# Two edits in the output stage of a gated encoder layer: which queue issues some stores, and where some loads stand in the queue

## The chip, the cores and the metric

The kernel runs on one core of a Trainium2 chip. The metric is the time of one execution in microseconds (us), lower is better. The time before is the median of three executions.

A core has a matrix engine (PE, with its weight loads shown as PEld), a vector engine (DVE), a scalar engine (ACT), GpSimd (POOL) and SyncE (SP). Each engine works off its own list of instructions in order. A DMA transfer is issued by an instruction in such a list: the engine that issues it waits until the data and the buffer are ready, and everything behind it in the same list waits too. The transfers themselves run on 16 DMA engines.

## The reference

One encoder layer over 1024 rows of width 2048. What matters here is its end: the merged branches times the output weights, a row norm, a gain, and the sum with the input.

```python
o = merged @ w_out                                   # (1024, 2048) @ (2048, 2048)
return x + gate[:, None] * rmsnorm(o, post_g)        # rmsnorm: rows scaled by 1 / sqrt(mean of squares + eps)
```

All is float32. Each matmul operand is split into a high and a low half, and three products stand for one. The squares of a whole row of `o` are needed before any element of the row can be finished.

## The kernel before

The large matmuls are done by a Strassen scheme of seven products for each 2x2 arrangement of blocks. The last stage, the output stage, is four calls of `out_pair(half, i, op, between, after)`: `half` is the half of the rows (rows 0 to 511, then 512 to 1023), and `i` picks a 512-wide column block out of each half of the columns. So each call makes, in seven products, the blocks of four row tiles (T, 128 rows each) by two column blocks (n). The calls come in the order (0,0), (0,1), (1,0), (1,1). One product is 48 matmuls of 128x512.

The weights of a product come in four loads of 512 KB (`wr`, L1185 for sums of weights kept in scratch, L1188 for `w_out` itself), into a ring of four buffers. A buffer is free again when its two halves have been split by ACT (`whi`, L95) and DVE (`wlo`, L96). So each product's weights are loaded about one product ahead. All of these loads are issued by SP.

A finished block is multiplied by the gain on DVE (L1284) in `result`. Of the calls for the first half, (0,1) keeps its eight blocks in SBUF (`held`), and (0,0) puts its eight blocks into a scratch tensor `o_d` (store at L1288, eight stores of 256 KB).

When a row's squares are complete, the rows of the first half are finished during (1,0) and the beginning of (1,1). `first_rows(T, n)` gives two steps for each of 16 blocks: `fetch` loads the block back from `o_d` if it is not held (L1353, eight loads `mo<-o_d`), and the block of `x` (L1220); `put_out` has DVE compute the final block in place (L1215) and stores it to the output (L1216). The tiles of these steps are a ring of eight places, used in turn: the blocks that come from `o_d` take the places 0, 2, 4, 6 and again 0, 2, 4, 6, so that a later load into a place must wait until the earlier block in that place has been stored. The steps are called from `between_10` and `between_11`, twice in each product; a step calls `fetch` of one block and then `put_out` of the block two earlier. The blocks of the second half are finished by `third_block` and at the very end of (1,1), with `finish_block` too.

The order of instructions within one engine's list is not the order of the code: a scheduler simulates the program and puts an instruction into its engine's list when it takes its inputs and buffers to be ready, earlier code first. `keep(ins)` (L90) is the exception: it adds an order without a wait, so that `ins` stands in its engine's list behind the instruction that the code traced last on that engine. It sets only this lower bound.

In the code, `load` and `store` are both `nc.sync.dma_start`, so loads and stores stand in the one list of SP.

Of the kernel before, what the change touches and what calls it, by code (L numbers as in the profile page):

```python
# [20 lines left out]
P = 128  # L21
# [21 lines left out]
def encoder_layer(ctx: ExitStack, tc: tile.TileContext, x, c, table, w_ada, b_ada, pre_g,  # L43
# [15 lines left out]
    nc = tc.nc  # L59
# [30 lines left out]
    def keep(ins):  # L90

        tc.keep_in_program_order(ins)
# [14 lines left out]
    load = nc.sync.dma_start  # L107
    store = nc.sync.dma_start
# [24 lines left out]
    o_d = dram.tile([S // 2, D], F32, name="o_d")  # L133
# [218 lines left out]
    for r0, src in ((0, c[0]), (16, b_ada[0, 0:D]), (32, b_ada[0, D:2 * D]),  # L352
                    (48, pre_g[0]), (64, b_merge[0]), (96, pool_scale[0])):
        n = src.shape[0] // P
# [421 lines left out]
    held = {}  # L776
# [421 lines left out]
    xrow, held = {}, {}  # L1198

    def rows_of(T, n):  # L1200
        return out[T * P:(T + 1) * P, n * 512:(n + 1) * 512]

    def square(src, T, n):
        nc.scalar.activation(bank("at", "junk"), src, AF.Square, accum_out=ssq[:, T, n:n + 1])

    def row_scale(T):
        s_ = const.tile([P, 3], F32, tag="st", name=uid("st"), bufs=4)
        nc.vector.tensor_reduce(s_[:, 0:1], ssq[:, T], op=ALU.add, axis=AX.X)
        nc.scalar.activation(s_[:, 1:2], s_[:, 0:1], AF.Sqrt, bias=eps_t, scale=1.0 / D)
        nc.vector.reciprocal(s_[:, 2:3], s_[:, 1:2])  # L1210
        return s_[:, 2:3]

    def finish_block(T, n, scale):
        r = held.pop((T, n))
        keep(nc.vector.scalar_tensor_tensor(r, r, scale, xrow.pop((T, n)), op0=ALU.mult, op1=ALU.add))  # L1215
        store(rows_of(T, n), r)  # L1216

    def fetch_x_block(T, n, tile_of):
        xrow[T, n] = tile_of("xr")
        load(xrow[T, n], x[T * P:(T + 1) * P, n * 512:(n + 1) * 512])  # L1220
# [7 lines left out]
    def out_pair(half, i, op, between, after=None):  # L1228
# [50 lines left out]
        def result(blk, t, src, dst):  # L1279

            T, nh = half * 4 + (int(blk[1]) - 1) * 2 + t, int(blk[0]) - 1
            n = 2 * nh + i
            square(src, T, n)
            nc.vector.tensor_tensor(dst, src, g[nh], ALU.mult)  # L1284
            if stays:
                held[T, n] = dst
            else:
                store(o_d[T * P:(T + 1) * P, n * 512:(n + 1) * 512], dst)  # L1288

        def kept(tag):  # L1290

# [14 lines left out]
        for t in range(2):  # L1306
            result("11", t, bx[t], c11[t])
        product("A22", "T4", bv)
        for t in range(2):
            add(u2[t], bv[t], u2[t])  # L1310
            result("21", t, u2[t], u2[t])
# [7 lines left out]
        for t in range(2):  # L1319
            add(p7[t], p7[t], u4[t])  # L1320
            result("22", t, p7[t], p7[t])
# [8 lines left out]
        for t in range(2):  # L1330
            for j, w in enumerate(ws):
                out_mm(bz[t], op, "B22", j, t, w, False, j == len(ws) - 1)
            result("12", t, bz[t], c12[t])
            scale = row_scale(6 + t)
            for n in (0, 2, 3, 1):
                finish_block(6 + t, n, scale)

    nextm, nextt2 = [], {}
    scales = {}
# [4 lines left out]
    def first_rows(T, n):  # L1344

        def place(name):
            ring.rotate(-1)
            return ring[-1]

        def fetch():  # L1350
            if (T, n) not in held:
                held[T, n] = place("fo")
                load(held[T, n], o_d[T * P:(T + 1) * P, n * 512:(n + 1) * 512])  # L1353
            fetch_x_block(T, n, place)

        def put_out():
            if T not in scales:
                scales[T] = row_scale(T)
            finish_block(T, n, scales[T])

        return fetch, put_out

# [52 lines left out]
    def third_block():  # L1415
        assert not side
        for T in (4, 5):
            scale = row_scale(T)
            for b in range(4):
                finish_block(T, b, scale)  # L1420
# [43 lines left out]
```

## Time and profile before

| | |
|---|---|
| median of 3 executions | 2125.57 us (2125.16 to 2127.92) |
| the profiled execution | 2127.43 us, its span 2125.6 us |
| PE busy | 2091.7 us, 98% of the span |
| DVE, ACT busy | 1537.8 us, 1109.0 us |
| POOL busy | 7.5 us |
| output stage | from about 1812 us to the end |
| DMA issues of the stage that the change touches | 8 stores to `o_d`, 8 loads from it, 16 stores of first-half blocks |

Times in the profile count from the start of the span. A line of the timeline has the start, the duration, the engine, the line of the kernel, the operation, and what it writes and reads. "SPq" is SP's list: the row of a DMA there is its issue and not its transfer; a DMA that had to wait is shown where it was issued at last. A bracket [0.96 <-ACT whi L95] is idle time of the engine before the instruction and what ended it. In the view of waits, "SPq L1353 <- DMA out_dram<-mo" reads: SP stood at line 1353 until a transfer from `mo` to the output had landed; then the sum, the number of times, and the longest.

### The profile page before, as it was taken

How to read it: one execution, taken by the hardware profiler on the slowest of the kernel's cores; microseconds unless marked ns; L12 is line 12 of the kernel's file. 1: busy time of each engine (PE TensorE's matmuls, PEld its weight loads, DVE VectorE, ACT ScalarE, POOL GpSimd, SP SyncE). 2: the span in 40 equal slices, each digit the busy share in tenths (PEclk: the TensorE clock that was granted, in tenths of full speed). 3: DMA queues.
4: the chain of work that ended last, by engine and by line, in shares of the span. 5: the costliest groups of instructions: out<-in, count | busy, mean ns of one | idle time of the engine just before them, and what ended most of it. 6: DMA issues, size and time to landing. Idle time of an engine off the chain costs nothing.

```text
span 2125.6 us, 28919 instructions
## 1 busy us (share of the span) xinstructions
PE 2091.7 (98%) x9567; PEld 1715.3 (81%) x9567; DVE 1537.8 (72%) x2754; ACT 1109.0 (52%) x2102; POOL 7.5 (0%) x66
## 2 busy tenths in 40 slices
PE   6999999999999999999999999999999999999998
PEld 4588888887888888888888888888788888878876
DVE  5786667777547676677777678866957977879667
ACT  5654444444474544665655544333645644768554
POOL 0000000000000000000000000000000000000000
PEclk9999999999999999999999999999999999999999
DMA  9886566899676356544545476666745556686896
GB/s 328 272 269 216 186 207 222 303 307 318 223 232 204 122 177 204 169 158 161 198 148 166 151 243 226 212 219 193 249 157 173 174 200 201 227 291 223 299 311 233
DMA packets 303254, 466.10 MB, mean 219 GB/s; under 512 B 23882, under 2 KB 144866, under 8 KB 303104
## 3 DMA queue, kind: packets, MB, share of 16 engines
q1 hardware_dynamic: 301648, 462.02, 65.9%
q0 software_dynamic: 1120, 2.19, 0.3%
q8 instruction: 75, 1.23, 0.2%
q14 instruction: 75, 0.61, 0.1%
q10 hardware_dynamic: 336, 0.06, 0.0%
HBM read 340.41 MB, written 125.85 MB: 219 GB/s over the span
## 4 chain that ended last, share of the span: by engine, by line
PE 87%; DVE 5%; DMA 5%; issue 1%; ACT 1%; SPq 0%; ACTq 0%; DVEq 0%
PE Z L235 29%; PE V L235 19%; PE X L235 19%; DMA raw<-in_w_merge_dram 2%; PE Z L1194 2%; PE Z L1195 2%; PE Z L1196 2%; PE V L1194 1%; PE V L1196 1%; PE V L1195 1%; PE GEMV L455 1%; DVE wlo L96 1%; PE X L1194 1%; PE X L1196 1%; PE X L1195 1%
## 5 line engine op out<-in xcount | busy, mean ns | idle before, releaser
L95 ACT ACTIVATE whi<-raw 128x512 fp32r<-128x512 f32 (+1 forms) x528 | 321.8, 610 | 527.1 <-PE Z L235 262.3
L96 DVE TENSOR_TENSOR wlo<-raw,whi 128x512 fp32r<-128x512 f32 (+1 forms) x528 | 347.6, 662 | 164.3 <-PE Z L235 129.2
L96 DVE TENSOR_TENSOR wlo<-wr,whi 128x512 fp32r<-128x512 f32 x224 | 151.3, 689 | 62.3 <-ACT whi L95 59.7
L95 ACT ACTIVATE whi<-wr 128x512 fp32r<-128x512 f32 x224 | 138.7, 629 | 96.4 <-DVE wlo L96 33.5
L102 DVE TENSOR_TENSOR raw<-raw,raw 128x512 f32<-128x512 f32 x80 | 55.2, 691 | 106.6 <-DMA raw<-in_w_merge_dram 78.2
L235 PE MATMUL V<-T3h,whi 128*128 128x512 f32 x336 | 92.1, 393 | 0.5 <-DVE u L102 0.5
L235 PE MATMUL V<-T4l,whi 128*128 128x512 f32 x336 | 91.2, 390 | 0.9 <-DVE T4l L96 0.8
L235 PE MATMUL X<-B11h,whi 128*128 128x512 f32 x336 | 92.0, 392 | 0.0
L235 PE MATMUL Z<-T2h,whi 128*128 128x512 f32 x336 | 91.6, 392 | 0.1
L95 ACT ACTIVATE whi<-ws 128x512 fp32r<-128x512 f32 (+1 forms) x88 | 53.7, 611 | 72.6 <-PE X L235 66.5
L235 PE MATMUL Z<-T1h,whi 128*128 128x512 f32 x336 | 91.6, 390 | 0.0
L235 PE MATMUL Z<-B22h,whi 128*128 128x512 f32 x336 | 91.6, 392 | 0.0
L235 PE MATMUL X<-B21h,whi 128*128 128x512 f32 x336 | 91.2, 391 | 0.0
L235 PE MATMUL V<-T4h,whi 128*128 128x512 f32 x336 | 91.2, 391 | 0.0
L235 PE MATMUL Z<-T2h,wlo 128*128 128x512 f32 x336 | 90.8, 390 | 0.2 <-DVE wlo L96 0.2
L235 PE MATMUL X<-B11l,whi 128*128 128x512 f32 x336 | 90.9, 390 | 0.0
L235 PE MATMUL Z<-T1l,whi 128*128 128x512 f32 x336 | 90.8, 390 | 0.0
L235 PE MATMUL Z<-B22l,whi 128*128 128x512 f32 x336 | 90.7, 390 | 0.0
L235 PE MATMUL X<-B11h,wlo 128*128 128x512 f32 x336 | 90.7, 390 | 0.0
L235 PE MATMUL V<-T3l,whi 128*128 128x512 f32 x336 | 90.7, 390 | 0.0
L235 PE MATMUL X<-B21l,whi 128*128 128x512 f32 x336 | 90.6, 389 | 0.0
L235 PE MATMUL Z<-T1h,wlo 128*128 128x512 f32 x336 | 90.6, 389 | 0.0
(308 smaller groups left out, 4811.8 us busy)
## 6 DMA issues: line engine op xcount, KB each, us to landing
part<-part_d SPq DMA_DIRECT2D x136, 256.0 KB, 4.8
ada<-in_w_ada_dram SPq DMA_DIRECT2D x128, 256.0 KB, 5.4
raw<-in_w_in_dram SPq DMA_DIRECT2D x64, 512.0 KB, 4.0
raw<-in_w_merge_dram SPq DMA_DIRECT2D x64, 512.0 KB, 5.7
wr<-ws_dS SPq DMA_DIRECT2D x64, 512.0 KB, 5.2
wr<-in_w_out_dram SPq DMA_DIRECT2D x48, 512.0 KB, 5.2
proj_d<-part SPq DMA_DIRECT2D x68, 256.0 KB, 2.2
sw<-in_w_out_dram SPq DMA_DIRECT2D x64, 256.0 KB, 5.5
```

The costliest lines, as they stand in the source:

```text
L95: ins = (nc.scalar.activation(hi, src, AF.Copy), nc.vector.tensor_tensor(lo, src, f32(hi), ALU.subtract))
L96: nc.vector.tensor_tensor(lo, src, f32(hi), ALU.subtract))
L102: return (eng or nc.vector).tensor_tensor(o, a, b, ALU.add)
L235: nc.tensor.matmul(ps, w_[:, i], op[mov][j][m_], start=fresh and i == 0 and n == 0, stop=i == nj - 1 and n == 2, skip_group_check=True)
L455: ins = nc.tensor.matmul(pv[g:g + 32, :], scz[:, kc, :], tile_of(kc), start=kc < 4, stop=kc >= 12, tile_position=(0, g))
L1194: nc.tensor.matmul(pb, hi, w[0], start=first, stop=False, skip_group_check=True)
L1195: nc.tensor.matmul(pb, lo, w[0], start=False, stop=False, skip_group_check=True)
L1196: nc.tensor.matmul(pb, hi, w[1], start=False, stop=last, skip_group_check=True)
```

## The change

The diff has three parts.

- The eight stores of `result` to `o_d` are issued by GpSimd and not by SP.
- `finish_block` takes the store as an argument. `put_out` of `first_rows` passes GpSimd's, so the 16 stores of first-half blocks go to GpSimd too. The other callers, `third_block` and the end of (1,1), keep SP.
- The eight loads from `o_d` in `fetch` get `keep`: each stands in SP's list behind the instruction traced just before it on SP. The blocks of `x` beside them are loaded as before, without it.

```diff
-    def finish_block(T, n, scale):
+    def finish_block(T, n, scale, store=store):
         r = held.pop((T, n))
         keep(nc.vector.scalar_tensor_tensor(r, r, scale, xrow.pop((T, n)), op0=ALU.mult, op1=ALU.add))
         store(rows_of(T, n), r)
...
             if stays:
                 held[T, n] = dst
             else:
-                store(o_d[T * P:(T + 1) * P, n * 512:(n + 1) * 512], dst)
+                nc.gpsimd.dma_start(o_d[T * P:(T + 1) * P, n * 512:(n + 1) * 512], dst)
...
             if (T, n) not in held:
                 held[T, n] = place("fo")
-                load(held[T, n], o_d[T * P:(T + 1) * P, n * 512:(n + 1) * 512])
+                keep(load(held[T, n], o_d[T * P:(T + 1) * P, n * 512:(n + 1) * 512]))
             fetch_x_block(T, n, place)
...
             if T not in scales:
                 scales[T] = row_scale(T)
-            finish_block(T, n, scales[T])
+            finish_block(T, n, scales[T], nc.gpsimd.dma_start)
```

## The prediction

> **What bounds the kernel now.** I read the page first, then the engines' timeline in the output stage, then the waits of SP's list and the chain.
>
> ```profile
> span 2125.6 us, 28919 instructions
> PE 2091.7 (98%) x9567; PEld 1715.3 (81%) x9567; DVE 1537.8 (72%) x2754; ACT 1109.0 (52%) x2102; POOL 7.5 (0%) x66
> ```
>
> PE is the bound. An edit outside the matmuls can win only what PE stands still, or what follows its last matmul. In the output stage the timeline of PE shows three such places:
>
> ```profile
> 1893.58 0.39 PE L1196 MATMUL X<-wlo,mh 128*128 128x512 f32 x1
> 1895.34 0.50 PE L1194 MATMUL V<-whi,mh 128*128 128x512 f32 x1 [1.37 <-ACT whi L95]
> ...
> 2050.63 0.39 PE L1195 MATMUL V<-whi,ml 128*128 128x512 f32 x1
> 2050.86 0.39 PE L1196 MATMUL V<-wlo,mh 128*128 128x512 f32 x1
> 2052.20 0.50 PE L1194 MATMUL V<-whi,mh 128*128 128x512 f32 x1 [0.96 <-ACT whi L95]
> 2052.54 0.40 PE L1195 MATMUL V<-whi,ml 128*128 128x512 f32 x1
> ...
> 2104.26 0.39 PE L1196 MATMUL Z<-wlo,mh 128*128 128x512 f32 x1
> 2105.74 0.50 PE L1194 MATMUL Z<-whi,mh 128*128 128x512 f32 x1 [1.09 <-ACT u L1276]
> ```
>
> Matmuls start 0.23 us apart when nothing is missing (2050.63 to 2050.86). Start to start, the three places take 1.76, 1.34 and 1.48 us, so they lose 1.5, 1.1 and 1.25 us. Behind a stall the pace comes back slowly (2052.20 to 2052.54 is 0.34); with three such steps each, that is another 0.3 us. The first two wait for a weight tile, the third for ACT's copy of a product. Now why the weights were late. The waits of SP from 1820 to 2126 us:
>
> ```profile
> SPq L1353 <- DMA out_dram<-mo: 14.2, 4, 4.5
> SPq L1216 <- DVE mo L1215: 8.0, 10, 1.8
> ```
>
> The first row is the key: four times the load of a kept result (L1353) stood in SP's list until the store of an earlier block from the same ring place had landed, 3.6 us each. SP's timeline shows what stood behind:
>
> ```profile
> 2019.32 0.35 SPq L1216 DMA_DIRECT2D out_dram<-mo  x1
> ...
> 2023.70 0.32 SPq L1353 DMA_DIRECT2D mo<-o_d  x1
> ...
> 2024.59 0.38 SPq L1185 DMA_DIRECT2D wr<-ws_dS  x1
> ...
> 2028.94 0.33 SPq L1353 DMA_DIRECT2D mo<-o_d  x1
> ...
> 2036.56 0.33 SPq L1353 DMA_DIRECT2D mo<-o_d  x1
> 2036.98 1.29 SPq L1188 DMA_DIRECT2D wr<-in_w_out_dram  x1
> 2038.36 0.42 SPq L1216 DMA_DIRECT2D out_dram<-mo  x1
> ...
> 2043.91 0.33 SPq L1353 DMA_DIRECT2D mo<-o_d  x1
> ...
> 2044.83 1.65 SPq L1185 DMA_DIRECT2D wr<-ws_dS  x3
> ```
>
> The four stand at 2023.70, 2028.94, 2036.56 and 2043.91, weight loads (`wr`) and further stores (2038.36) stand behind them. The chain takes the stall at 2052 back through exactly these:
>
> ```profile
> 2036.98 6.17 DMA wr<-in_w_out_dram
> ...
> 2044.83 6.59 DMA wr<-ws_dS
> ```
>
> **The change, part by part.**
>
> *Stores of first rows to GpSimd (16).* SP loses 16 issues of 0.35 us, which are not on the path by themselves. What counts is that a store no longer stands behind a waiting load. DVE's timeline has the block of the store of 2038.36:
>
> ```profile
> 2033.63 0.75 DVE L1215 SCALAR_TENSOR_TENSOR mo<-mo,st 128x512 f32<-128x512 f32 x1
> ```
>
> It was done at 2034.4 and stored 4.0 us later, and the load of 2043.91 had to wait for that store. From GpSimd, which has nothing else to do here (7.5 us busy in all), it can go at 2034.4. With the 5.5 us that it took from 2038.36 to the load that it released at 2043.91, it lands at 2039.9, and the weight load of 2044.83 goes up to 4 us earlier. It needs only 1.1 us. So the 1.1 us at 2052 go, even if the load of 2036.56 stays where it is: gain 1.1.
>
> *Stores to `o_d` to GpSimd (8).* The first stall is of this kind. SP's list and the chain there:
>
> ```profile
> 1879.34 2.01 SPq L1179 DMA_DIRECT2D m<-m_d  x4
> ...
> 1885.01 0.32 SPq L1288 DMA_DIRECT2D o_d<-u  x1
> ...
> 1885.85 0.95 SPq L1240 DMA_DIRECT2D pg<-pg_d  x2
> ...
> 1880.32 6.71 DMA m<-m_d
> 1887.10 7.46 DMA wr<-ws_dS
> ```
>
> The weight load of 1887.10 was let go when a load of `m` issued at 1880.32 had landed, eight transfers back in the list. Two of these eight are stores to `o_d`, the second at 1885.01. Without them the eighth back is the first `m` load, of 1879.34, one us earlier. The gain loads (`pg`, L1240) stand ahead as well and need the gain tile that DVE reads until the block of the second store is made, at 1885.0; two issues later, at about 1886.0 and not at 1887.1, the weight load can go by both. I take 1.0 of the 1.5 us; between nothing (if its transfer is held up as before by what is under way) and 1.5.
>
> *The eight pinned loads.* Each now stands behind the instruction traced ahead of it on SP. Their group in the view of the tile `o_d`:
>
> ```profile
> L1353 SPq DMA_DIRECT2D mo<-o_d x8: 320/379/498, 1968.0 to 2043.9; - x8
> ```
>
> For the first four the bound is a weight load of the product in hand, which SP issues about one product (48 x 0.227 = 10.9 us) ahead of use. They move later, the first from 1968.0 by some 25 us; the first block made from such a load is stored at 2019.32, so 50 us of room cover that, and these loads waited for no store. The one of 2023.70 has its bound, an earlier weight load, ahead of it already: it stays. The one of 2028.94 moves behind the last of the four weight loads of the next call, that of 2036.98; by then its store has landed and it waits for nothing. The last two are bound only by the `x` load ahead of them and may stay between weight loads. So the pins take out one of four waits and leave three. I count no gain of their own and no loss. If the moved load came late after all, DVE would stand at L1215 with the splits of the weights behind it, and PE would wait as at 2052.
>
> *What the move costs.* GpSimd must make the descriptors, and its stores may land later. The trace has only three GpSimd transfers, beside many of SP:
>
> ```profile
> oh<-in_onehot_dram POOLq DMA_DIRECT2D x1, 66.0 KB, 4.0
> line_d<-bl POOLq DMA_DIRECT2D x1, 16.0 KB, 4.8
> bias_d<-line_d POOLq DMA_DIRECT2D x1, 2048.0 KB, 16.8
> out_dram<-mo SPq DMA_DIRECT2D x16, 256.0 KB, 4.2
> tab<-in_rel_bias_table_dram SPq DMA_DIRECT2D x1, 1.0 KB, 3.5
> ```
>
> Against SP's small load, the small ones take 0.5 to 1.3 us more. The large one is 2.1 us for each 256 KB, no slower than SP's 4.2 in all. So a store from GpSimd lands between 1.3 us later and, as it does not queue behind SP's loads, perhaps 1 us earlier; I take 0.5 later. It only matters for the three loads that still wait. The nearest is the weight load of 2024.59, with this much room:
>
> ```profile
> 2026.46 0.39 PE L1194 MATMUL Z<-whi,mh 128*128 128x512 f32 x1
> 2031.29 0.63 ACT L95 ACTIVATE whi<-wr 128x512 fp32r<-128x512 f32 x1 [1.11 <-DMA wr<-ws_dS]
> ```
>
> It had landed by 2031.29. PE reads its first tile after 36 matmuls of the product that begins at 2026.46, so at about 2034.6. Less 0.63 for the split, 2.7 us are spare: 0.5 or 1.3 costs nothing. The Trainium skill (DMA: Bandwidth & Descriptors, Specifications) has first bytes after about 1 us from GpSimd and 0.6 us from SP; by these the store lands 0.4 us later, an estimate, and the sum stays.
>
> *Sum.* 1.1 + 1.0 = 2.1 us off the span, 2123.5 us. The work behind PE's last matmul keeps SP's stores and follows PE as it is. The profiled execution took 2127.43 us, 1.9 above the median of 2125.57; I take the 2.1 off the median: **2123.5 us**. 0.2% of it, 4.25 us, is about what a measurement of this kernel can tell from no change.
>
> **The rivals.**
>
> *Slower: GpSimd's stores land much later, and SP stands longer in front of weights.* The place is the load of 2023.70 and again that of 2043.91. If a store lands x later, the spare 2.7 us at 2034.6 are used up and x - 2.7 is lost; at 2052 the store starts 4.0 us earlier and 1.1 were lost before, so the loss there changes by x - 4. With 1.0 won at 1895, no gain is left from x of about 3.9. At x = 6, a landing time of over 10 us, it is 3.3 + 2.0 - 1.0 = 4.3 slower: 2129.9 us. For it speaks that DVE is busy 72% and that nothing in this trace shows a store of a whole tile from GpSimd; against it, the three rows above. Chance 0.22, a tenth of it within 0.2%.
>
> *No gain: the DMA engines set the time, not the list.* From the windows:
>
> ```profile
> 2035.00:2040.00 5.00, 5.00 (x24) 4.14 (x23) 3.65 (x6) 3.37 (x8) 0.00 (x0) 1.00 0.69 230
> 2050.00:2080.00 30.00, 29.04 (x127) 23.45 (x126) 16.68 (x25) 16.54 (x29) 0.00 (x0) 1.00 0.99 350
> 2069.69 1.15 ACT L95 ACTIVATE whi<-wr 128x512 fp32r<-128x512 f32 x2 [2.87 <-DMA wr<-in_w_out_dram]
> ```
>
> From 2050 to 2080 they are 99% busy, and for the weights of 2069.69 ACT had already stood idle 2.87 us. If PE comes 1.1 us earlier and the transfers do not, the stall only moves there, and at 1895 likewise: 2125.6. Against it, the engines are only 69% busy while SP stands still, 1.5 us of work that could be moved forward. The Trainium skill (Trainium Kernel Development and Optimization, Key Constraints) says that DMAs from several engines' queues share the same 16 DMA engines, and that issuing from several saves only the issue time. By that rule the move is worth nothing and the time is 2125.6 again; the waits of L1353 speak against it, since SP's list loses far more by standing than by issuing. Chance 0.19; this takes in that the change leaves the waits in SP's list as they were.
>
> *Faster by more than 0.2%.* All three stalls go with their slow restarts: 1.5 + 1.1 + 1.25 + 3 x 0.3 = 4.75, 2120.8 us. The two for weights could; for the third, the shifted order would have to bring ACT's copy forward. Nothing in the change touches ACT's copy at 2105. Chance 0.12.
>
> **How the numbers follow.** Forecast 0.47, no gain 0.19, slower 0.22, faster 0.12. Slower by over 0.2%: 0.20. Faster by over 0.2%: 0.12. Within: 0.47 + 0.19 + 0.02 = 0.68. The range runs from the faster rival's 2120.8, a little below, to 2130.5, a little above the slower rival's 2129.9; about half of each lies outside. The likeliest case alone runs from 2122 (both stalls for weights gone with their restarts, 1.5 + 1.1 + 0.6 = 3.2, and some tenths more) to 2125 (a little of the first alone).
>
> **What would show it.** In the profile after: SP's wait at L1353 for stores falls from 14.2 us in four to three waits of 10 us or less, and no wait at L1216 before 2100 us remains; PE's waits for ACT's split in the product beginning at 2048 is gone, that at 1895 is below 0.6 us; landing of GpSimd's stores has a median of 4 to 6 us. I am wrong if these stores land after 8 us or more, if new PE waits for weights show between 2030 and 2075, or if DVE waits for a kept result.

## The result, and the profile after

The changed kernel takes 2122.9 us in the median of 22 executions (2119.2 to 2125.2), the kernel before 2125.5 us in 22 taken beside it. The ratio of the two is 0.9987, with a 95% interval of 0.9981 to 0.9993: 2.8 us faster, between 1.5 and 4.0 us. The forecast was 2123.5 us, so the size is right within what can be measured. That the parts of the sum were not all of the right size is told below.

The profiled execution has a shorter span than the median would suggest. The first lines of its page:

```profile
span 2120.7 us, 28959 instructions
...
PE 2089.0 (99%) x9567; PEld 1715.1 (81%) x9567; DVE 1538.7 (73%) x2754; ACT 1109.5 (52%) x2102; POOL 20.4 (1%) x90
```

That is 4.9 us below the 2125.6 us of before. Spans of single executions are a poor measure here: the time at which the output stage begins lies anywhere from 1801.9 to 1809.0 us in the profiles of this case, although all of these programs issue the same instructions in the same order up to about 1850 us. It is better to measure the stage by itself, from the start of its first matmul (first start of the X group at L1194) to the start of its last (last start of the Z group at L1196). This first matmul is at 1803.8 us before, somewhat earlier than the "about 1812 us" of the table ahead of the prediction. The rows of the kernel before, from the views of these lines:

```profile
L1194 PE MATMUL X<-whi,mh x128: 389/389/391, 1803.8 to 2081.9; 128*128 128x512 f32 x128
...
L1196 PE MATMUL Z<-wlo,mh x192: 388/389/501, 1828.8 to 2116.5; 128*128 128x512 f32 x192
```

And of the changed kernel:

```profile
L1194 PE MATMUL X<-whi,mh x128: 389/389/391, 1803.6 to 2078.2; 128*128 128x512 f32 x128
...
L1196 PE MATMUL Z<-wlo,mh x192: 388/389/398, 1828.6 to 2111.6; 128*128 128x512 f32 x192
```

Before it is 2116.5 - 1803.8 = 312.7 us, after 2111.6 - 1803.6 = 308.0 us. What follows the last matmul is 9.1 us in both. So 4.7 of the 4.9 us lie between the matmuls of the stage, and the waits of PE in the stage of the changed kernel are an empty list: all three places where PE stood still are gone. (The third is missing in a second profile of the kernel before as well, as the first experiment shows, so its absence here is not put down to the change.) The window around the first place, before and then in the changed kernel (its columns: PE, PEld, DVE, ACT, POOL busy, then clock, share of the DMA engines, GB/s):

```profile
1876.00:1896.00 20.00, 18.63 (x82) 14.84 (x80) 9.10 (x15) 8.77 (x17) 0.00 (x0) 1.00 0.96 317
1876.00:1896.00 20.00, 20.00 (x90) 16.58 (x89) 13.24 (x21) 11.54 (x21) 1.56 (x3) 1.00 0.94 333
```

SP's list there in the changed kernel, and GpSimd's two stores:

```profile
1878.73 0.38 SPq L1188 DMA_DIRECT2D wr<-in_w_out_dram  x1
1879.22 0.89 SPq L1240 DMA_DIRECT2D pg<-pg_d  x2
1881.40 8.52 SPq L1185 DMA_DIRECT2D wr<-ws_dS  x4
```

```profile
1883.30 0.54 POOL L1288 DMA_DIRECT2D o_d<-u  x1 [6.83 <-DVE u L1284]
1885.10 0.54 POOL L1288 DMA_DIRECT2D o_d<-u  x1 [1.26 <-DVE u L1284]
```

The weight load that left at 1887.10 leaves at 1881.40, as soon as its buffer is free. The loads of `m` are not between the stores any more: with the stores out of SP's list the scheduler spread them over the weight loads before. The stores wait in GpSimd's list, where no load stands behind them.

Around the second place, SP's list of the changed kernel:

```profile
2022.90 0.33 SPq L1353 DMA_DIRECT2D mo<-o_d  x1
...
2029.52 0.37 SPq L1188 DMA_DIRECT2D wr<-in_w_out_dram  x1
2033.49 0.34 SPq L1353 DMA_DIRECT2D mo<-o_d  x1
2033.94 0.82 SPq L1188 DMA_DIRECT2D wr<-in_w_out_dram  x1
2034.81 0.46 SPq L1353 DMA_DIRECT2D mo<-o_d  x1
...
2035.93 0.33 SPq L1353 DMA_DIRECT2D mo<-o_d  x1
2036.35 1.09 SPq L1185 DMA_DIRECT2D wr<-ws_dS  x2
```

Two of the four loads of kept results still stand before weight loads (2022.90 and 2033.49), but the fourth goes at 2035.93 and not at 2043.91, and the weight load behind it at about 2036.9 and not at 2044.83. SP's waits from 1820 to 2090 us:

```profile
SPq L1353 <- DMA out_dram<-mo: 7.6, 2, 4.1
SPq L1240 <- DMA out_dram<-c: 4.7, 2, 3.6
```

The first was 14.2 us in four. The second is new: loads of the gain into tiles whose blocks GpSimd stores wait for these stores to land. PE waits for nothing that stands behind them.

### The profile page after: what moved, and what is told of

It reads as the page before. It is cut to its first block, busy times and chain, and to the rows that moved or that the text cites. A ratio compares the mean times of both kernels' runs of the same rounds, so it can differ in the third digit from the quotient of the medians.

```text
span 2120.7 us, 28959 instructions
## 1 busy us (share of the span) xinstructions
PE 2089.0 (99%) x9567; PEld 1715.1 (81%) x9567; DVE 1538.7 (73%) x2754; ACT 1109.5 (52%) x2102; POOL 20.4 (1%) x90
## 4 chain that ended last, share of the span: by engine, by line
PE 90%; DVE 5%; DMA 3%; issue 1%; ACT 1%; SPq 0%; ACTq 0%; DVEq 0%
PE Z L235 30%; PE X L235 20%; PE V L235 20%; PE Z L1194 2%; PE Z L1195 2%; PE Z L1196 2%; PE V L1196 1%; PE X L1196 1%; PE X L1195 1%; PE V L1195 1%; PE V L1194 1%; PE X L1194 1%; PE GEMV L455 1%; DMA raw<-in_w_merge_dram 1%; DVE wlo L96 1%; PE PT L905 1%
## 5 line engine op out<-in xcount | busy, mean ns | idle before, releaser
L96 DVE TENSOR_TENSOR wlo<-wr,whi 128x512 fp32r<-128x512 f32 x224 | 151.0, 688 | 55.9 <-ACT whi L95 49.8
```

Of the source, the lines that this page charges most:

```text
L96: nc.vector.tensor_tensor(lo, src, f32(hi), ALU.subtract))
```

## The experiments

In the diffs, a line with - is that of the kernel named in the text. The stage is measured as above in each run's profile; the ratio is to the kernel before, run beside it.

### The kernel before once more

> The kernel before once more, unchanged, to see how far its own stalls and time move from execution to execution. If the stalls belong to the order of SP's list, PE again stands still at about 1895 and 2052 us for 1 us or more each; the third, at about 2105, was put down to ACT's copy of a product and may come or go. If the stalls are chance, one or both of the first two are missing. Time the same as before within 1 us.

Ratio 1.0002, interval 0.9993 to 1.0011. PE's timeline:

```profile
1895.94 0.39 PE L1196 MATMUL X<-wlo,mh 128*128 128x512 f32 x1
1897.38 0.50 PE L1194 MATMUL V<-whi,mh 128*128 128x512 f32 x1 [1.05 <-ACT whi L95]
...
2052.90 0.39 PE L1196 MATMUL V<-wlo,mh 128*128 128x512 f32 x1
2054.17 0.50 PE L1194 MATMUL V<-whi,mh 128*128 128x512 f32 x1 [0.88 <-ACT whi L95]
```

The two stalls for weights are there again, 1.2 and 1.0 us (1.44 and 1.27 less 0.23). The third is not; the stage is 310.9 us. So the first two belong to the program, and the third comes and goes. The stage begins 2.4 us later than in the first profile of the same program (1806.2 against 1803.8), and the span of 2126.2 us shows nothing of the shorter stage.

### Only the stores to scratch on GpSimd

```diff
-                store(o_d[T * P:(T + 1) * P, n * 512:(n + 1) * 512], dst)
+                nc.gpsimd.dma_start(o_d[T * P:(T + 1) * P, n * 512:(n + 1) * 512], dst)
```

> Only the eight stores to the scratch tensor go to GpSimd; first rows' stores stay on SP, no load is pinned. Theory (a store that waits holds up the loads behind it in SP's list): the stall at about 1895 is gone, the one at about 2052 stays at 1 us or more, SP still waits four times at the loads of kept results for about 14 us; time 1 to 2 us lower. Rival (the pins or the other stores carry the gain): the stall at 1895 stays, time as before.

Ratio 0.9987 (0.9978 to 0.9996), stage 310.3 us. PE does not wait at 1895. It waits three times later on, for 0.5 us each; the third wait, at 2103.12, is for ACT's copy, and the first two are these:

```profile
2048.87 0.40 PE L1196 MATMUL V<-wlo,mh 128*128 128x512 f32 x1
2049.65 0.50 PE L1194 MATMUL V<-whi,mh 128*128 128x512 f32 x1 [0.38 <-ACT whi L95]
...
2068.89 0.39 PE L1196 MATMUL Z<-wlo,mh 128*128 128x512 f32 x1
2069.58 0.50 PE L1194 MATMUL X<-whi,mh 128*128 128x512 f32 x1 [0.30 <-ACT whi L95]
```

The first stall belongs to these stores, as expected. SP's wait at L1353 is still 13.7 us in four, and PE still stands at the second place, for 0.55 us (0.78 less 0.23) and not 1 us or more. The stall at 2069.58 is at the place that the prediction's rival of no gain named: PE comes earlier than the weights there, and loses 0.5 us. It does not show that rival's cause, that the DMA engines and not the list set the time. The chain of this run takes the late weights back through two transfers:

```profile
2053.28 7.68 DMA xr<-in_x_dram
...
2061.03 7.77 DMA wr<-in_w_out_dram
```

The weight load was issued only when the load of `x` issued at 2053.28 had landed, so SP's list held it too. And in the changed kernel the DMA engines are as busy from 2050 to 2080 us (0.96 of the time, 0.97 here), and PE does not wait.

### Only the stores of first rows on GpSimd

```diff
-            finish_block(T, n, scales[T])
+            finish_block(T, n, scales[T], nc.gpsimd.dma_start)
```

> Only the 16 stores of first rows go to GpSimd; scratch stores stay on SP, no load is pinned. Theory: the stall at about 1895 stays at 1.5 us, the one at about 2052 is gone, the wait at the loads of kept results falls from 14 us to about 10 us; time about 1 us lower. Rival (pins are needed because GpSimd's stores land later): the stall at 2052 stays or grows, the wait stays at 14 us or more, time as before or higher.

Ratio 0.9996 (0.9986 to 1.0005), stage 310.1 us. One stall is left in the stage:

```profile
1898.17 0.39 PE L1196 MATMUL X<-wlo,mh 128*128 128x512 f32 x1
1900.40 0.50 PE L1194 MATMUL V<-whi,mh 128*128 128x512 f32 x1 [1.85 <-ACT whi L95]
```

It is the first, 2.0 us here. The second is gone, and SP's wait at L1353 for stores is 8.7 us in two. SP's list shows that one of the two long waits is still there:

```profile
2042.04 0.34 SPq L1353 DMA_DIRECT2D mo<-o_d  x1
...
2043.95 0.42 SPq L1353 DMA_DIRECT2D mo<-o_d  x1
2044.45 0.87 SPq L1185 DMA_DIRECT2D wr<-ws_dS  x1
```

The load of 2042.04 stood for 4.9 us, with weight loads behind it, but the next and last one did not wait for a store. This is what the prediction said of the load of 2036.56: it may stay, and the stall goes all the same. Pins are not needed for it.

### Only the pins

```diff
-                load(held[T, n], o_d[T * P:(T + 1) * P, n * 512:(n + 1) * 512])
+                keep(load(held[T, n], o_d[T * P:(T + 1) * P, n * 512:(n + 1) * 512]))
```

> Only the loads of kept results are pinned; all stores stay on SP. Theory: two of the four waits stay, and a store still stands behind each; the stall at about 1895 stays, the one at about 2052 shrinks by half at most; time at most 0.5 us lower. Rival (the pins carry the gain): the stall at 2052 is gone, time 1.5 us lower or more.

Ratio 0.9995 (0.9986 to 1.0003), stage 309.6 us. Again the first stall is the only one:

```profile
1893.34 0.39 PE L1196 MATMUL X<-wlo,mh 128*128 128x512 f32 x1
1895.02 0.50 PE L1194 MATMUL V<-whi,mh 128*128 128x512 f32 x1 [1.30 <-ACT whi L95]
```

Here the theory fell: the pins alone take away the whole second stall, and SP's wait at L1353 for stores falls to 3.1 us, less than in the changed kernel. The pinned load goes behind the weight load, the next weight load and store come earlier, and the later waits shrink with it. The second stall hung on a chain of four waits, each of which delayed the store for the next; one link taken out was enough. The rival is right in that much, but the time cannot tell: its interval takes in no change.

### Both stores, no pins

Of the changed kernel, the load goes back to `load(...)` without `keep`.

> The change without its pins: both kinds of stores on GpSimd, the loads of kept results free in SP's list. Theory (the pins and the move of the first rows' stores each remove the stall at about 2052, so one of them is enough): no stall of 1 us at 1895 or 2052, the output stage from its first to its last matmul 308 to 309.5 us as in the changed kernel (307.9) and not 311 to 313 as before; time 2 to 3 us below before. Rival (GpSimd's stores land later, so the pins are needed with them): a stall of 0.7 us or more between 2030 and 2075, stage 310 us or more.

Ratio 0.999 (0.9981 to 0.9999), stage 307.9 us, no stall.

### Scratch stores and pins, stores of first rows on SP

Of the changed kernel, `put_out` calls `finish_block(T, n, scales[T])` again.

> The change without the move of the first rows' stores: scratch stores on GpSimd, loads pinned, first rows' stores on SP. Theory: stage 308 to 309 us, no stall of 1 us, SP's wait at the loads of kept results about 3 us (as with the pins alone) and not 7.6 us as in the changed kernel; time 2 to 3.5 us below before, the same as the changed kernel. Rival (the move of the first rows' stores is needed once PE comes earlier at 1895): a stall of 0.7 us or more at about 2050 or 2069, stage 310 us or more.

Ratio 0.9983 (0.9974 to 0.9992), stage 307.7 us, no stall; SP's wait at L1353 for stores is 5.6 us, where about 3 were expected. So the changed kernel without the move of the first rows' stores is no slower.

Together these five say: the move of the scratch stores removes the first stall; the second is removed by the move of the first rows' stores or by the pins, and either makes the other superfluous. The first stall is there in the four profiles in which SP issues the scratch stores and in none of the eight others of this case. All of this is read from the stalls in the profiles, one for most kernels. The times bear out the scratch stores alone: by themselves they have the ratio of the whole change, 0.9987, while the first rows' stores alone and the pins alone do not differ from before beyond their intervals.

### The loads of kept results on GpSimd too

```diff
-                keep(load(held[T, n], o_d[T * P:(T + 1) * P, n * 512:(n + 1) * 512]))
+                nc.gpsimd.dma_start(held[T, n], o_d[T * P:(T + 1) * P, n * 512:(n + 1) * 512])
```

> The changed kernel with the eight loads of kept results on GpSimd as well, behind the stores they wait for, and no pins: SP waits for no store at all in first rows. Theory: the remaining 7.6 us of SP's waits cost PE nothing, so the stage stays at 308 us and the time at that of the changed kernel. Rival (these waits still cost): stage below 307.5 us, time 0.5 us or more below the changed kernel. A third outcome, GpSimd's loads land so late that DVE waits at the final block: stage 309 us or more.

Ratio 0.9991 (0.9982 to 1.0), stage 308.2 us. SP waits nowhere at L1353 or L1216 before the last stores. GpSimd waits there instead, 26.4 us in four, and nobody feels it. So the 7.6 us of SP's waits that the changed kernel has left cost nothing.

### The stores issued by ACT

```diff
-                nc.gpsimd.dma_start(o_d[T * P:(T + 1) * P, n * 512:(n + 1) * 512], dst)
+                nc.scalar.dma_start(o_d[T * P:(T + 1) * P, n * 512:(n + 1) * 512], dst)
...
-            finish_block(T, n, scales[T], nc.gpsimd.dma_start)
+            finish_block(T, n, scales[T], nc.scalar.dma_start)
```

> The changed kernel with the 24 stores issued by ACT and not by GpSimd. Theory (what counts is what stands behind a waiting store): in ACT's list the splits of the weights stand behind each store until DVE has made the block, up to 1 us each; ACT shows waits for DVE blocks at the two store lines, PE stalls come back, stage 309 us or more, time 1 to 5 us above the changed kernel. Rival (it is enough that the stores leave SP's list): stage 308 us, time as the changed kernel.

Ratio 0.9991 (0.9983 to 1.0), stage 309.1 us. Both theories are half right. The time is within the noise of the changed kernel's, so the price of 1 to 5 us was too high; the stage is 1.1 us longer, by one stall at 1873.72, where PE waits for ACT's copy. ACT's timeline shows why:

```profile
1872.04 1.15 ACT L95 ACTIVATE whi<-wr 128x512 fp32r<-128x512 f32 x2 [1.22 <-DMA wr<-ws_dS]
1873.09 0.58 ACT L1276 ACTIVATE u<-Z 128x512 f32<-128x512 f32 x1
```

The copy stood in ACT's list behind the split of a weight load that had not landed. Whether the moved stores made that load late stays open. The view of ACT's waits lists none at the two store lines, which speaks against the theory. But earlier on SP's gain load (L1240) waited until one of the stores that ACT had issued had landed:

```profile
SPq L1240 <- DMA o_d<-c: 3.2, 1, 3.2
```

It was issued at 1856.65, and the weight load behind it at 1857.06, where the changed kernel issues the same one at 1854.03. So this run shows neither that the stores in ACT's list hurt nor that they do not. It does show the same wait as the third stall: in the kernel before, ACT's timeline at 2104 has the same two steps:

```profile
2104.06 1.15 ACT L95 ACTIVATE whi<-wr 128x512 fp32r<-128x512 f32 x2 [0.97 <-DMA wr<-ws_dS]
2105.11 1.06 ACT L1276 ACTIVATE u<-Z 128x512 f32<-128x512 f32 x2
```

The order alone does not make a stall. In the changed kernel, too, the copy stands behind such a split (2099.09, after 0.88 us of waiting for weights), and PE does not wait.

### The changed kernel once more

> The changed kernel once more, unchanged. If the order of the lists sets the stalls, PE again waits nowhere for weights in the output stage and the stage is 307.7 to 308.5 us; the third kind of stall (PE waiting for ACT's copy of a product) may show once, of up to 1.3 us. If the first profile was a lucky one, a stall of 1 us at 1895 or 2050 is back. Time 2 to 3.5 us below before.

Ratio 0.9983 (0.9974 to 0.9992), median 2122.8 us. The stage is 307.7 us, PE waits for nothing in it. The first profile was no lucky one.

### The copy ahead of the splits

Of the changed kernel, at the last product:

```diff
-            last = split_weights("S4", ring=False, pin=(6, 7))
-            ws = [next(last) for _ in range(6)]
+            last = split_weights("S4", ring=False, pin=(4, 5, 6, 7))
+            ws = [next(last) for _ in range(4)]
```

> The changed kernel with one edit at the last product: ACT copies the last-but-one product before it splits the fifth and sixth weight tile, and not behind them. It tests what the third stall of before was. Theory (ACT's list held the copy behind the split of a weight load that was still under way): PE cannot wait for that copy for more than its own 1 us, but the two splits come later and PE may wait for them; stage 308 to 309 us, time the same as the changed kernel. Rival (the copy itself was slow, or the work behind the last matmul gains): stage or tail shorter by 0.5 us or more than in the changed kernel.

Ratio 0.9995 (0.9986 to 1.0004), stage 308.9 us. PE does not wait for the copy, but 0.4 us for a split that now comes later:

```profile
2106.50 0.50 PE L1196 MATMUL Z<-wlo,mh 128*128 128x512 f32 x1 [0.24 <-DVE wlo L96]
```

So the later splits have a price, as the theory has it. That the earlier copy takes a wait away is not shown, since PE does not wait for the copy in the changed kernel either. The tail, from the start of the last matmul to the end, is 8.7 us, 0.4 shorter; the time is no better than the changed kernel's (medians of 2124.9 and 2122.8 us, run side by side). No run here beats the changed kernel beyond its noise.

## Why the prediction was right, point by point

**The bound and the places.** The changed kernel is without the three stalls, and the work behind the last matmul is as long as before. Only the first two were won by the change; the third was in one of two profiles of the kernel before. The stage went from 312.7 and 310.9 us (two profiles) to 308.0 and 307.7. The mean difference is 4.0 us, at the upper end of the interval of the times, 1.5 to 4.0; against the profile without the third stall it is 2.9 to 3.2 us.

**The sum, 2.1 us.** It is a little low against the 2.8 us measured, though inside the interval. One reason is the term for the first stall, below. The other is that the sum leaves out the slow restarts, which the prediction itself put at 0.3 us for each stall: in the second profile of the kernel before the two stalls add up to 2.2 us, and the stage is 2.9 to 3.2 us longer than in the changed kernel.

**The second stall, 1.1 us.** Right as a number, and the way was right as far as it went: the store of the block finished at 2034.4 no longer stands behind a waiting load, and the weight load behind the last wait leaves 8 us earlier. What the prediction left out is that the pins do the same by another way. Its "no gain of their own" for the pins is wrong for the pins alone and right beside the moved stores.

**The first stall, 1.0 of 1.5 us.** The mechanism was right, the term was too small: all of it went. The step that failed is the bound by the gain loads. They were thought to need a tile that DVE reads until 1885.0; in the changed kernel they are issued at 1879.22, 5 us before DVE begins that block (1884.13). So the weight load was bound by its own buffer alone and left at 1881.40, not at 1886.0.

**The cost of the move.** The stores from GpSimd were to land 0.5 us later, with a median of 4 to 6 us. The 4.2 us for SP that the prediction compared with is a median of two kinds: of the sixteen stores from `mo`, eight are of first rows and land in 5.5 us, and eight come after 2095 us and land in 2.4. Like with like, the 16 stores of first rows (L1216, 1960 to 2060 us) in the kernel before, the changed kernel and the kernel with the stores on ACT:

```profile
DMA to landing us min/median/max: 3.1/5.5/8.2
DMA to landing us min/median/max: 3.6/6.2/7.8
DMA to landing us min/median/max: 3.0/5.5/9.0
```

And the eight stores to scratch (L1288), in the same order:

```profile
DMA to landing us min/median/max: 3.3/4.5/5.4
DMA to landing us min/median/max: 5.2/6.2/6.9
DMA to landing us min/median/max: 5.7/6.8/7.5
```

So GpSimd's stores of first rows land 0.7 us later, close to the 0.5 that was taken, and its scratch stores 1.7 us later. Both medians are 6.2 us, just above the 4 to 6 that was to be seen. Only the stores of first rows free a place that a load of a kept result waits for, and the 2.7 us to spare at the nearest weight load covered their 0.7. The slower rival needed 3.9 us and more.

**The rivals.** "No gain" named a place where a stall of 0.5 us came up in one run, though not, as far as is shown, by its cause; in the changed kernel there was none. Around the first stall the DMA engines were 0.96 busy before and 0.94 after and moved 317 and 333 GB/s, so they were as full as before; what changed is which transfers came first. The rule from the Trainium skill (Trainium Kernel Development and Optimization, Key Constraints) that issuing from several engines saves only the issue time does not cover this case. The two stores ahead of the first stall took 0.64 us to issue, and the weight load behind them leaves 5.7 us earlier: what was won is the time that SP's list stood, not the issues. "Faster by more than 0.2%" is what the first profile looks like, 4.9 us; the times, 1.5 to 4.0 us, say that it is not. Its third part, the stall behind ACT's copy, was there in one of two profiles of the kernel before.

**What would have shown it wrong.** DVE waits for no kept result, and no weight wait came up between 2030 and 2075. SP's wait at L1353 was to be three waits of 10 us or less in all; it is two of 7.6 us (three of 7.6 in the second profile). One wait of 1.8 us at L1216 is left before 2100 us, where none was to be; it is a store of SP's at 2099.32, which the change leaves with SP.

## What to carry to other kernels

Read a DMA queue as an instruction list: a store that waits for its data, or a load that waits for its buffer, delays every load behind it, however free the DMA engines are. Put transfers that wait for compute into the list of an engine that has nothing else to do (ACT, which has other work, gave no different time here), and keep loads that feed the bound engine in a list where they wait only for their own buffers. When several edits act on one chain of waits, test each alone, since one may make the others superfluous; and measure the stage in the profile, since the time of the whole kernel moved by several us between executions here, and the stage of the changed kernel by 0.3 us between its two profiles.

## What the runs showed of the hardware that was not expected

The scratch stores land later from either of the two other lists, so this is not GpSimd's way of issuing alone. ACT takes 0.33 us for an issue where GpSimd takes 0.54, and its scratch stores take 6.8 us to land against 6.2 from GpSimd and 4.5 from SP. The stores of first rows show hardly any of this: 5.5 us from SP and from ACT, 6.2 from GpSimd. Whether a second queue gets a smaller share beside SP's loads, or the loads that are now earlier take the engines, was not tried and stays open.

GpSimd's 24 stores did not slow DVE. Its splits of weights, from the pages of before and after:

```profile
L96 DVE TENSOR_TENSOR wlo<-wr,whi 128x512 fp32r<-128x512 f32 x224 | 151.3, 689 | 62.3 <-ACT whi L95 59.7
```

```profile
L96 DVE TENSOR_TENSOR wlo<-wr,whi 128x512 fp32r<-128x512 f32 x224 | 151.0, 688 | 55.9 <-ACT whi L95 49.8
```

Their mean is 689 and 688 ns, and the idle time before them fell from 62.3 to 55.9 us.
